# Norms on column strips, totals by transposes, decay exponents without a mask product

## The chip, the cores and the metric

The kernel runs on one core of one Trainium2 chip. The metric is device time in microseconds, the median of the runs of one build. A core has TensorE (matmul, PE in the profile, with its weight loads as PEld), VectorE (DVE), ScalarE (ACT), GpSimd (POOL) and SyncE (SP, which issues most transfers here). Each engine works through its own instructions in order, and the engines wait for each other by semaphores.

## The reference

One layer of a hybrid backbone: 1024 latent tokens and 256 context tokens of width 1024. All that the change touches lies in the modulation and in the gated delta rule.

```python
mod_x = silu(c) @ w_ada + b_ada                     # six vectors of 1024: shift, scale, gate, twice
px = modulate(rms_norm(x), sh1, sc1) @ w_in         # one projection, columns split into two groups
...
q = l2_normalize(silu(conv(q))) * 128 ** -0.5       # 4 heads of 128
k = l2_normalize(silu(conv(k)))
gam = cumsum(g)                                     # per chunk, per direction
decay = exp(where(tril, gam[:, None] - gam[None, :], -inf))
a_mat = eye + where(strict, (beta * k) @ k.T * decay, 0)
u, w = solve(a_mat, v * beta), solve(a_mat, k * beta * exp(gam))
qk = where(tril, q @ k.T * decay, 0)
o = (q * exp(gam)) @ S + qk @ (u - w @ S)           # scanned over chunks, forward and backward, summed
...
x = x + g1 * (concat(delta, neighbourhood_attention) @ w_out)
x = x + g2 * (silu(gate) * up) @ w_ffn_out          # gate, up from modulate(rms_norm(x), sh2, sc2) @ w_ffn_in
```

Here `tril` is the lower triangle of a chunk, and for the backward scan the upper one.

## The kernel before, in words

Every large product is made of three products of split operands in a fast 32-bit format (high by high, high by low, low by high), into 128x512 banks of the accumulator: `mm_part` (L422) for the projection, L1418 and L1761 for the feed-forward part.

**Order.** From about 150 to 500 us the program goes through a list of projection blocks (q, k, v of the delta rule, nq and nk of the attention, wide blocks for the rest). Between the main products of a block it steps generators that carry all other work in pieces: `modulation`, `block_inverses`, `preps`, and the `norm` and `finish` of the block before. A scheduler with a cost model of its own then decides the final order on each engine, within the data dependences; a few instructions are pinned by `keep_in_program_order`. So an edit in one place can shift rows in another. Three more stages follow: the scan with attention (500 to 775 us), the output projection and the feed-forward part.

**Modulation.** For each of eight groups of 512 columns, VectorE adds up eight scaled tiles of weights into `acc2` (128x512, L238). `reduce` (L220 to L225) then sums over the 128 partitions with four matmuls of one moving column, and VectorE adds the bias. Four groups run in the projection stage, two at about 826 us, two between 1175 and 1245 us.

**A query block's norm (L500 to L507).** The squares `r` (128 x 1024) are summed over partitions by eight matmuls that have 128 squares' columns as stationary operand and a column of ones as moving one, which gives the sums with tokens on partitions; VectorE copies them to `SQ`.

**A query block's finish (L558 to L583).** The transposed keys are loaded from DRAM into `kTh`, the products of keys and queries of each chunk are made on TensorE (L570), ScalarE copies them to `kk` (L571), and one store puts them into `qk_d` (L583), unmasked.

**preps (L970 to L1070).** For each of ten chunk numbers, a pair of chunks (one for each direction) is worked on. `fetch` loads the keys' products `kk` (L991), the inverses' blocks `xc` (L992) and the query products `at` (L996). `prep` makes the exponents' operands `rg` on VectorE (L1008), copies blocks to `fx` on ScalarE (L1012), multiplies with the triangles on TensorE (L1020, two products), adds a third product that brings −1e30 to every position outside the triangle (L1023), and takes the exponential `e` (L1028). Masked positions of `e` are thus zero, and VectorE multiplies `kk` and `at` by it (L1031, L1036). GpSimd copies blocks into `y` (L1034); TensorE multiplies with `fx` (L1044) and then, block row by block row, with `y` (L1055).

The buffers of `preps` take the memory of the block inverses, so the first `rg` waits until the last of the inverses (`ut` and `WK`, L952 to L957) has been stored to `x_d`.

Of the kernel before, what the change touches and what calls it, by code (L numbers as in the profile page):

```python
# [88 lines left out]
def hybrid(ctx, tc, a, dbg):  # L89
# [15 lines left out]
    def lasting(name, shape, dt=F32):  # L105
        return persist.tile(shape, dt, name=name, tag=name)

    prm = lasting("prm", [128, 64])
    ones = lasting("ones", [128, 128])
    bias = lasting("bias", [128, 8])  # L110
    modp = lasting("modp", [128, 48])
# [11 lines left out]
    act.dma_start(sel, a["sel"])  # L123
    cst = const("cst", [128, NCONST])
    M = [cst[:, i * 128:(i + 1) * 128] for i in range(4)] + [ones]
    mc = [cst[:, 512 + i * 32:512 + (i + 1) * 32] for i in range(4)]
    ident = M[C_ID]
    n1w, n2w, bada = prm[:, 0:8], prm[:, 8:16], prm[:, 16:64]
# [7 lines left out]
    b_eps, b_naq = bias[:, 0:1], bias[:, 1:2]  # L136
    mr = const("mr", [128, 5, 128], F32R)

# [5 lines left out]
    kk_d = dram.tile([128, NCH, 4, 128], F32, name="kk_d", tag="kk_d")  # L144
    qk_d = dram.tile([128, 8, 4, 128], F32, name="qk_d", tag="qk_d")
    nv_d = dram.tile([T, 512], F32, name="nv_d", tag="nv_d")
# [61 lines left out]
    def modulation(adp, qs, bank, bufs=4, sums=2):  # L208
# [11 lines left out]
        def reduce(q, acc2):  # L220
            p = bank()
            for b in range(4):
                pe.matmul(p[:, b:b + 1], acc2[:, b * 128:(b + 1) * 128], ones[:, 0:1], start=True, stop=True)  # L223
            s = slice(16 + q * 4, 20 + q * 4)
            dve.tensor_tensor(modp[:, s], p[:, 0:4], bada[:, s], OP.add)  # L225

# [165 lines left out]
    with ExitStack() as bs:  # L392
# [32 lines left out]
        class Block:  # L425
# [64 lines left out]
            def norm(self):  # L490
# [8 lines left out]
                if kind == "q":  # L499
                    sp.dma_start(qT_d[:, :, i], acc[:, t0:].rearrange("p (c t) -> p c t", t=128))  # L500
                    p = bank()
                    for c in range(8):
                        m = pe.matmul(p[:, c:c + 1], r[:, t0 + c * 128:t0 + (c + 1) * 128], M[C_ONE][:, 0:1],
                                      start=True, stop=True)
                        if not c:
                            tc.keep_in_program_order(m)
                    dve.tensor_copy(SQ[:, :, i], p[:, 0:8])  # L507
                    return
# [30 lines left out]
            def finish(self):  # L539
# [22 lines left out]
                if kind in "kq":  # L562
# [10 lines left out]
                    if kind == "k":  # L573
# [4 lines left out]
                        for b in range(4):  # L578
                            s = slice(b * 32, b * 32 + 32)
                            pool.tensor_copy(KKc.rearrange("p (c h) i -> p c h i", h=4)[s, :, i], kk[s, :, s])  # L580
                            pool.memset(kk[s, :, s], 0.0)
                    dst = kk_d if kind == "k" else qk_d
                    sp.dma_start(dst[:, :, i], kk[:, c0:])  # L583

# [90 lines left out]
        with ExitStack() as xs:  # L675
# [18 lines left out]
            for j in range(3):  # L694
                load_ada(j)
            sp.dma_start(cst, a["cst"])
            sp.dma_start(masks, a["masks"])
# [43 lines left out]
            with tc.manual_schedule(engines={mybir.EngineType.PE, mybir.EngineType.DVE, mybir.EngineType.Activation}):  # L741
# [40 lines left out]
                for k in range(1, KT):  # L782
                    if k == 3:
                        ascope.close()
                        h_tiles(pools(bs, "hp2", "right"), 4)
                    if k + 1 < KT:
                        normed_tile(k + 1)
                    for j, b in enumerate(first):
                        b.mm([k])
                        for q in AHEAD.get((k, j), ()):  # L790
                            if q in rows:
                                column(q)
                            else:
                                ada(q, act.copy)
                    if k == 5:
                        act.copy(mr[:, 4], ident)
                        act.copy(mr[:, 0:4], masks)
# [4 lines left out]
        adp = pools(late, "adp", "left")  # L802
        mneg = adp.tile([128, 2, 128], F32R, name="mneg", tag="mneg")
        for d in range(2):
            act.mul(mneg[:, d], mr[:, d].bitcast(F32), -1.0e30)
        first_half = ExitStack()
# [161 lines left out]
        def preps():  # L968

            first_half.close()  # L970
            with ExitStack() as gs:
# [13 lines left out]
                def fetch(i):  # L985

                    got = []
                    for d in range(2):
                        c = ORDER[d][i]
                        kk, xc = work("kk", 6), pp.tile([128, 2, 4, 32], F32, name="xc", tag="xc", bufs=4)  # L990
                        sp.dma_start(kk, kk_d[:, c])  # L991
                        sp.dma_start(xc, x_d[:, d, :, c * 4:c * 4 + 4])  # L992
                        at = None
                        if c >= 2:
                            at = work("at", 4)
                            sp.dma_start(at, qk_d[:, c - 2])  # L996
                        got.append((d, c, kk, xc, at))
                    return i, got

                def prep(i, got):  # L1000
# [16 lines left out]
                    for d, c, kk, xc, at in got:  # L1017
                        p = bank("pr")
                        for j in range(2):
                            m = pe.matmul(p, mr[:, d], fl(rgs[2 * d + j]), start=j == 0, stop=False)  # L1020
                            if i == 0:
                                tc.keep_in_program_order(m)
                        pe.matmul(p, mr[:, 4], mneg[:, d].rearrange("p (o i) -> p o i", o=1).to_broadcast(  # L1023
                            [128, 4, 128]), start=False, stop=True)
                        e = work("e", 2)
# [818 lines left out]
```

## Time and profile before

| | us |
| --- | --- |
| median of three runs (smallest, largest) | 1490.75 (1489.34, 1491.34) |
| profiled execution | 1493.29 |
| its span, first to last instruction | 1491.4 |
| TensorE busy | 1454.2 |
| VectorE busy | 997.8 |
| ScalarE busy | 706.0 |
| GpSimd busy | 92.4 |

The mean granted TensorE clock is 0.997. A "record" is one TensorE instruction of the trace: a matmul of ordinary 32-bit numbers leaves two, a transpose or a product in the fast format one. Matmuls are pipelined, so a duration reaches into the next instruction's.

### The profile page before, as it was taken

How to read it: one execution, taken by the hardware profiler on the slowest of the kernel's cores; microseconds unless marked ns; L12 is line 12 of the kernel's file. 1: busy time of each engine (PE TensorE's matmuls, PEld its weight loads, DVE VectorE, ACT ScalarE, POOL GpSimd, SP SyncE). 2: the span in 40 equal slices, each digit the busy share in tenths (PEclk: the TensorE clock that was granted, in tenths of full speed). 3: DMA queues.
4: the chain of work that ended last, by engine and by line, in shares of the span. 5: the costliest groups of instructions: out<-in, count | busy, mean ns of one | idle time of the engine just before them, and what ended most of it. 6: DMA issues, size and time to landing. Idle time of an engine off the chain costs nothing. (4 is left out here: it accounts for less than half of the span.)

```text
span 1491.4 us, 23615 instructions
## 1 busy us (share of the span) xinstructions
PE 1454.2 (98%) x8708; PEld 1223.5 (82%) x8708; DVE 997.8 (67%) x1794; ACT 706.0 (47%) x1388; POOL 92.4 (6%) x168
## 2 busy tenths in 40 slices
PE   6999999999999989989999999999999999999998
PEld 3889898887898878888878888888888888888887
DVE  5783698865663547779966589755556556698652
ACT  5453544457653256667752374333333335355440
POOL 1033000202110001001100000000000000000000
PEclk9999999999999999999999999999999999999999
DMA  9265232877654489986349105333233335898742
GB/s 386 77 208 162 74 86 66 267 241 239 207 182 159 140 271 294 291 249 213 116 168 312 43 15 198 120 106 106 107 106 106 100 106 182 292 330 289 254 135 85
DMA packets 203091, 264.19 MB, mean 177 GB/s; under 512 B 15712, under 2 KB 111456, under 8 KB 201952
## 3 DMA queue, kind: packets, MB, share of 16 engines
q1 hardware_dynamic: 195376, 256.87, 53.2%
q10 hardware_dynamic: 7600, 5.81, 1.2%
q8 instruction: 69, 1.13, 0.3%
q14 instruction: 46, 0.38, 0.1%
HBM read 197.87 MB, written 68.94 MB: 179 GB/s over the span
## 5 line engine op out<-in xcount | busy, mean ns | idle before, releaser
L1479 ACT CAST uhi<-wq 128x512 fp32r<-128x512 f32 x101 | 61.3, 622 | 134.0 <-issue 84.7
L1479 ACT CAST uhi<-ws 128x512 fp32r<-128x512 f32 x91 | 54.0, 621 | 146.6 <-PE ps L1418 96.7
L422 PE MATMUL blk<-hh,whi 128*128 128x512 f32 (+1 forms) x410 | 120.3, 387 | 0.5 <-ACT kk L571 0.5
L422 PE MATMUL blk<-hl,whi 128*128 128x512 f32 (+1 forms) x410 | 114.3, 371 | 0.3 <-DVE hl L738 0.3
L618 PE MATMUL blk<-zw,hh 128*128 128x256 f32 (+1 forms) x576 | 112.6, 289 | 1.0 <-ACT cr L470 1.0
L422 PE MATMUL blk<-hh,wlo 128*128 128x512 f32 (+1 forms) x410 | 112.5, 369 | 0.0
L1480 DVE TENSOR_TENSOR ulo<-wq,uhi 128x512 fp32r<-128x512 f32 x101 | 67.9, 687 | 58.5 <-ACT uhi L1479 31.9
L1418 PE MATMUL ps<-hT,uhi 128*128 128x512 f32 x336 | 103.7, 390 | 0.0
L1418 PE MATMUL ps<-hT,ulo 128*128 128x512 f32 x336 | 103.5, 389 | 0.0
L1418 PE MATMUL ps<-lT,uhi 128*128 128x512 f32 x336 | 103.4, 389 | 0.0
L618 PEld LDWEIGHTS blk<-zw,hh 128*128 128x128 f32 x576 | 90.9, 189 | 4.1 <-ACT cr L470 1.4
L1418 PE MATMUL ps<-hB,uhi 128*128 128x512 f32 x288 | 89.1, 390 | 0.0
L1418 PE MATMUL ps<-lB,uhi 128*128 128x512 f32 x288 | 88.7, 389 | 0.0
L1418 PE MATMUL ps<-hB,ulo 128*128 128x512 f32 x288 | 88.7, 389 | 0.0
L422 PEld LDWEIGHTS blk<-hl,whi 128*128 128x128 f32 x410 | 71.2, 189 | 14.2 <-DVE hl L738 0.8
L422 PEld LDWEIGHTS blk<-hh,wlo 128*128 128x128 f32 x410 | 71.1, 188 | 13.7
L618 PE MATMUL blk<-zw,hl 128*128 128x256 f32 (+1 forms) x288 | 81.8, 284 | 0.0
L422 PEld LDWEIGHTS blk<-hh,whi 128*128 128x128 f32 x410 | 67.5, 190 | 15.4 <-issue 4.0
L1418 PEld LDWEIGHTS ps<-hT,ulo 128*128 128x128 f32 x336 | 63.1, 188 | 13.1
L1418 PEld LDWEIGHTS ps<-lT,uhi 128*128 128x128 f32 x336 | 63.1, 188 | 13.1
L1418 PEld LDWEIGHTS ps<-hT,uhi 128*128 128x128 f32 x336 | 62.9, 188 | 13.0
L316 DVE CUSTOM_DVE_ANT_0 ex<-sc,bt 128x640 f32<-128x640 f32 x64 | 52.5, 820 | 22.9 <-PE sc L310 17.5
(361 smaller groups left out, 3357.4 us busy)
## 6 DMA issues: line engine op xcount, KB each, us to landing
wq<-w_fo SPq DMA_DIRECT2D x99, 256.0 KB, 4.0
wq<-w_gu SPq DMA_DIRECT2D x88, 256.0 KB, 2.8
wad<-wa SPq DMA_DIRECT2D x64, 256.0 KB, 4.4
t_d<-g SPq DMA_DIRECT2D x22, 512.0 KB, 3.5
fr<-t_d SPq DMA_DIRECT2D x44, 256.0 KB, 5.0
bt<-rpb SPq DMA_DIRECT2D x48, 192.0 KB, 3.9
f_d<-g SPq DMA_DIRECT2D x33, 256.0 KB, 2.1
fr<-f_d SPq DMA_DIRECT2D x33, 256.0 KB, 4.1
```

The costliest lines, as they stand in the source:

```text
L316: dve.tensor_tensor_reduce(e, sc[:, u * 640:u * 640 + 640], bt, -1.0, 3.0e38, OP.add, OP.min, m[:, 0:1])
L422: pe.matmul(o, ww[:, k], xx[k][:, s], start=k == 0 and j == 0, stop=k == KT - 1 and j == 2)
L618: pe.matmul(p[:, :c1 - c0], x[k][:, s], ww[:, k, c0:c1], start=k == 0 and j == 0, stop=k == KT - 1 and j == 2)
L1418: pe.matmul(o, w[wi][:, k], x[xi][:, k], start=first and k == 0 and j == 0, stop=k == n - 1 and j == 2, skip_group_check=True)
L1479: act.copy(hi, self.raw[key])
L1480: dve.tensor_tensor(lo, self.raw[key], hi.bitcast(F32), OP.subtract)
```

## The change

**Totals.** Four transposes of `acc2` go into one 128x512 bank, VectorE sums each transposed block along its free axis into `modp`, and then adds the bias.

**Query norms.** Four matmuls have a 128x32 block of ones as stationary and 256 columns of squares as moving operand; each writes to another strip of 32 partitions of one bank. ScalarE copies the bank's first 256 columns to a buffer, two transposes bring the tokens onto partitions, and VectorE copies every 32nd column to `SQ`.

**Decays.** The third product and its operands are gone. The exponent is then zero outside the triangle, and `e` is one there. So what `e` multiplies has to be zero there already: three memsets per `kk` tile in `fetch` clear the 32-wide blocks outside the triangle (60 in all; the diagonal blocks were cleared before, by `finish` of the key blocks), and `finish` of the query blocks makes two masked copies of the products, for the forward direction into the `kTh` buffer and for the backward one in place, and stores both.

**The identity** gets a tile of its own with its own load, in persistent memory; the table of constants shrinks by as much.

```diff
         def reduce(q, acc2):
             p = bank()
             for b in range(4):
-                pe.matmul(p[:, b:b + 1], acc2[:, b * 128:(b + 1) * 128], ones[:, 0:1], start=True, stop=True)
+                pe.transpose(p[:, b * 128:(b + 1) * 128], acc2[:, b * 128:(b + 1) * 128], ident)
             s = slice(16 + q * 4, 20 + q * 4)
-            dve.tensor_tensor(modp[:, s], p[:, 0:4], bada[:, s], OP.add)
+            dve.tensor_reduce(modp[:, s], p.rearrange("p (b j) -> p b j", b=4), AX.X, OP.add)
+            dve.tensor_tensor(modp[:, s], modp[:, s], bada[:, s], OP.add)
...
                     p = bank()
-                    for c in range(8):
-                        m = pe.matmul(p[:, c:c + 1], r[:, t0 + c * 128:t0 + (c + 1) * 128], M[C_ONE][:, 0:1],
-                                      start=True, stop=True)
+                    for c in range(4):
+                        m = pe.matmul(p[32 * c:32 * c + 32, :256], M[C_ONE][:, 0:32],
+                                      r[:, t0 + c * 256:t0 + (c + 1) * 256], start=True, stop=True)
                         if not c:
                             tc.keep_in_program_order(m)
-                    dve.tensor_copy(SQ[:, :, i], p[:, 0:8])
+                    row = cp.tile([128, 272], F32, name="zt", tag="zt", bufs=2)
+                    act.copy(row[:, :256], p[:, :256])
+                    p = bank()
+                    for b in range(2):
+                        pe.transpose(p[:, b * 128:b * 128 + 128], row[:, b * 128:b * 128 + 128], ident)
+                    dve.tensor_copy(SQ[:, :, i].rearrange("p (s b) -> p s b", b=2),
+                                    p[:, :256].rearrange("p (b s j) -> p s b j", b=2, s=4)[:, :, :, 0])
                     return
...
-                    dst = kk_d if kind == "k" else qk_d
-                    sp.dma_start(dst[:, :, i], kk[:, c0:])
+                    if kind == "k":
+                        sp.dma_start(kk_d[:, :, i], kk)
+                        return
+                    for d, x in enumerate((kT.rearrange("p (c t) -> p c t", t=128), kk)):
+                        keep = M[C_LE + d].rearrange("p (o i) -> p o i", o=1).to_broadcast([128, NCH - c0, 128])
+                        dve.tensor_tensor(x[:, c0:], kk[:, c0:], keep, OP.mult)
+                        sp.dma_start(qk_d[d, :, :, i], x[:, c0:])
...
                         sp.dma_start(kk, kk_d[:, c])
+                        for b in range(3):
+                            rows, cols = (b, slice(32 * b + 32, 128)) if d else (b + 1, slice(0, 32 * b + 32))
+                            pool.memset(kk[q32[rows], :, cols], 0.0)
...
-                            sp.dma_start(at, qk_d[:, c - 2])
+                            sp.dma_start(at, qk_d[d, :, c - 2])
...
-                            m = pe.matmul(p, mr[:, d], fl(rgs[2 * d + j]), start=j == 0, stop=False)
+                            m = pe.matmul(p, mr[:, d], fl(rgs[2 * d + j]), start=j == 0, stop=j == 1)
                             if i == 0:
                                 tc.keep_in_program_order(m)
-                        pe.matmul(p, mr[:, 4], mneg[:, d].rearrange("p (o i) -> p o i", o=1).to_broadcast(
-                            [128, 4, 128]), start=False, stop=True)
```

The scheduler's order moves with it. TensorE before, at the first decays (L1020) of `preps`, 25 main products behind the second L570 group of the first query block. A row gives the line, the operation, out<-in, the shape, and how many follow each other:

```order
L422 MATMUL blk<-hh_131,whi 128x512
L1020 MATMUL pr<-rg,mr 128x512
L422 MATMUL blk<-hh_131,whi 128x512
L422 MATMUL blk<-hl_132,whi 128x512
L1020 MATMUL pr<-rg,mr 128x512
L1023 MATMUL pr<-mneg,mr 128x512
L1020 MATMUL pr<-rg,mr 128x512
L422 MATMUL blk<-hl_132,whi 128x512
L422 MATMUL blk<-hh_131,wlo 128x512
L1020 MATMUL pr<-rg,mr 128x512
L1023 MATMUL pr<-mneg,mr 128x512
```

The same place in the changed kernel (L422 is L423 there, L1020 is L1032):

```order
L423 MATMUL blk<-hh_467,wlo 128x512 x2
L1032 MATMUL pr<-rg,mr 128x512
L423 MATMUL blk<-hh_469,whi 128x512
L1032 MATMUL pr<-rg,mr 128x512
L423 MATMUL blk<-hh_469,whi 128x512
L423 MATMUL blk<-hl_470,whi 128x512
L1032 MATMUL pr<-rg,mr 128x512
L423 MATMUL blk<-hl_470,whi 128x512
L423 MATMUL blk<-hh_469,wlo 128x512
L1032 MATMUL pr<-rg,mr 128x512
```

The two mask products are gone, and the decays now stand 12 main products behind that L570 group in place of 25.

VectorE before, where the first `rg` is made (L478 is a tap of the convolution, L238 modulation's running sum, L507 the copy of a query norm):

```order
L507 COPY SQ<-m 128x8
L478 SCALAR_TENSOR_TENSOR cacc<-cr,cw,cacc 128x1023
L952 STREAM_TRANSPOSE ut<-WK 128x1280
L478 SCALAR_TENSOR_TENSOR cacc<-cr,cw,cacc 128x1023
L955 TENSOR_TENSOR WK<-WK,NB 128x1280
L478 SCALAR_TENSOR_TENSOR cacc<-cr,cw,cacc 128x1022
L238 SCALAR_TENSOR_TENSOR acc_2466<-wad,sc_100,acc_2466 128x512 x3
L1008 TENSOR_TENSOR rg<-GH,cst 128x512
```

And in the changed kernel (L478 is L479, L952 is L961, L1008 is L1020; the copy of the norm is L513):

```order
L961 STREAM_TRANSPOSE ut<-WK 128x1280
L479 SCALAR_TENSOR_TENSOR cacc<-cr,cw,cacc 128x1023
L964 TENSOR_TENSOR WK<-WK,NB 128x1280
L479 SCALAR_TENSOR_TENSOR cacc<-cr,cw,cacc 128x1023
L239 SCALAR_TENSOR_TENSOR acc_2465<-wad,sc_101,acc_2465 128x512
L1020 TENSOR_TENSOR rg<-GH,cst 128x512
L1020 TENSOR_TENSOR rg<-GL,cst 128x512
L1020 TENSOR_TENSOR rg<-GH,cst 128x512
L1020 TENSOR_TENSOR rg<-GL,cst 128x512
L479 SCALAR_TENSOR_TENSOR cacc<-cr,cw,cacc 128x1022
L513 COPY SQ<-m 128x8
L239 SCALAR_TENSOR_TENSOR acc_2465<-wad,sc_101,acc_2465 128x512
```

The copy of the norm and one tap no longer stand ahead of the transpose of the inverses, and two of the running sums ahead of `rg` are gone; two masked products of 128x1024 (L594) come soon behind.

GpSimd in the changed kernel, with buffer numbers, at the first pair of `preps` (before, only the copies to `y` stood there, which are L1034 before and L1044 now):

```order
L1044 COPY y00_2501<-xc_2512 32x4x32 x4
L1003 MEMSET kk_2511 32x4x32
L1003 MEMSET kk_2511 32x4x64
L1003 MEMSET kk_2511 32x4x96
L1003 MEMSET kk_2518 32x4x96
L1003 MEMSET kk_2518 32x4x64
L1003 MEMSET kk_2518 32x4x32
L1044 COPY y10_2502<-xc_2519 32x4x32 x4
```

Six memsets of two `kk` tiles stand between the copies of a pair.

More of the change, by code (lines that the diff above doesn't have):

```diff
@@ L109, in hybrid @@
     ones = lasting("ones", [128, 128])
+    ident = lasting("ident", [128, 128])
     bias = lasting("bias", [128, 8])
@@ L123, in hybrid @@
     act.dma_start(sel, a["sel"])
[L124 to L127, printed above, removed]
+    cst = const("cst", [128, NCONST - 128])
+    M = [ident] + [cst[:, i * 128:(i + 1) * 128] for i in range(3)] + [ones]
+    mc = [cst[:, 384 + i * 32:384 + (i + 1) * 32] for i in range(4)]
     n1w, n2w, bada = prm[:, 0:8], prm[:, 8:16], prm[:, 16:64]
@@ L136, in hybrid @@
     b_eps, b_naq = bias[:, 0:1], bias[:, 1:2]
-    mr = const("mr", [128, 5, 128], F32R)
+    mr = const("mr", [128, 4, 128], F32R)
     v_d = dram.tile([T, 512], F32, name="v_d", tag="v_d")
@@ L144, in hybrid @@
     kk_d = dram.tile([128, NCH, 4, 128], F32, name="kk_d", tag="kk_d")
-    qk_d = dram.tile([128, 8, 4, 128], F32, name="qk_d", tag="qk_d")
+    qk_d = dram.tile([2, 128, 8, 4, 128], F32, name="qk_d", tag="qk_d")
     nv_d = dram.tile([T, 512], F32, name="nv_d", tag="nv_d")
@@ L695, in hybrid @@
                 load_ada(j)
-            sp.dma_start(cst, a["cst"])
+            sp.dma_start(ident, a["cst"][:, 0:128])
+            sp.dma_start(cst, a["cst"][:, 128:])
             sp.dma_start(masks, a["masks"])
@@ L795, in hybrid @@
                     if k == 5:
-                        act.copy(mr[:, 4], ident)
                         act.copy(mr[:, 0:4], masks)
@@ L802, in hybrid @@
         adp = pools(late, "adp", "left")
-        mneg = adp.tile([128, 2, 128], F32R, name="mneg", tag="mneg")
-        for d in range(2):
-            act.mul(mneg[:, d], mr[:, d].bitcast(F32), -1.0e30)
         first_half = ExitStack()
```

## Prediction

> **What bounds the kernel now.** I read the page's first part, then the busy time by stage (one window per stage), then the timeline at the places that the change touches. The columns of a window row are: stretch, its length, busy us and instruction count of PE, weight loads, VectorE, ScalarE and GpSimd, granted clock, DMA share, GB/s.
>
> ```profile
> span 1491.4 us, 23615 instructions
> PE 1454.2 (98%) x8708; PEld 1223.5 (82%) x8708; DVE 997.8 (67%) x1794; ACT 706.0 (47%) x1388; POOL 92.4 (6%) x168
> 150.00:500.00 350.00, 350.00 (x2352) 296.20 (x2350) 241.85 (x326) 178.68 (x325) 36.76 (x88) 0.99 0.56 170
> 500.00:775.00 275.00, 256.28 (x2322) 226.33 (x2321) 193.95 (x555) 172.41 (x461) 25.98 (x36) 0.99 0.71 215
> ```
>
> TensorE sets the pace: 98% of the span, and 350.00 of 350.00 us in the stage that holds the whole change but four modulation totals. There a TensorE instruction taken away shortens the kernel by its issue interval, and work added to another engine costs nothing until TensorE waits for it. The scan stage has 18.7 us of TensorE idle time (275.00 − 256.28), but the change puts nothing in it except another order of the same instructions.
>
> **Mask products: removed.** The timeline rows are: start, duration, engine, line, operation, out<-in, count. Durations overlap, so I price by the distance between starts.
>
> ```profile
> L1023 PE MATMUL pr<-mneg,mr x20: 389/396/401, 281.6 to 456.6; 128*128 128x512 f32 x20
> 281.39 0.39 PE L1020 MATMUL pr<-rg,mr 128*128 128x512 f32 x1
> 281.62 0.40 PE L1023 MATMUL pr<-mneg,mr 128*128 128x512 f32 x1
> ```
>
> A 128x512 product takes 0.23 us of the engine's time (281.39 to 281.62), not its 0.396, and a pair 0.46. Twenty of them: 20 × 0.23 = **−4.6 us**.
>
> **Modulation totals: one-column products become transposes.** A total was four one-column matmuls, eight records.
>
> ```profile
> 260.00 0.95 PE L223 MATMUL m<-ones,acc 128*128 128x1 f32 x8
> 260.81 0.70 PE L422 MATMUL blk<-hl,whi 128*128 128x512 f32 x2
> 261.35 0.63 PE L422 MATMUL blk<-hh,wlo 128*128 128x512 f32 x2
> 78.58 1.25 PE L546 MATMUL m<-cst,cacc 128*128 128x128 f32 x10
> 79.59 0.48 PE L422 MATMUL blk<-hh,wlo 128*128 128x512 f32 x1
> 79.91 1.11 PE L570 MATMUL m<-cacc 128*128 128x128 f32 x8
> ```
>
> Before: 0.81 us (260.00 to 260.81), and the pair behind takes 0.54 (to 261.35) in place of 0.46, so 0.89. After: the ten transposes at 78.58 took 1.01, hence 0.10 each, and the product behind them 0.32 in place of 0.23, so 4 × 0.10 + 0.09 = 0.49. There are eight totals (four of them in the projection stage): 8 × 0.40 = **−3.2 us**.
>
> **Query norms on column strips.** A norm was eight one-column matmuls (16 records); it becomes four matmuls with a 32-column stationary and 256 moving columns, one for each strip of the output, then two transposes.
>
> ```profile
> 268.65 1.84 PE L503 MATMUL m<-ones,cr 128*128 128x1 f32 x16
> 270.35 0.72 PE L422 MATMUL blk<-hh,whi 128*128 128x512 f32 x2
> 270.91 0.63 PE L422 MATMUL blk<-hl,whi 128*128 128x512 f32 x2
> 24.96 1.07 PE L715 MATMUL pm<-wada,wide 128*32 128x256 f32 x16
> 25.96 0.73 PE L762 MATMUL pm<-whi 128*128 128x512 f32 x2
> 361.24 1.88 PE L511 MATMUL m<-cr,cst 128*128 128x512 f32 x4
> 294.74 0.44 PE L1055 MATMUL pr<-y,kk 128*32 128x32 f32 x8
> 295.11 0.73 PE L422 MATMUL blk<-hl,whi 128*128 128x512 f32 x2
> 295.68 0.62 PE L422 MATMUL blk<-hh,wlo 128*128 128x512 f32 x2
> ```
>
> Before: 1.70 (268.65 to 270.35), and 0.56 − 0.46 = 0.10 behind: 1.80. The nearest row to the new form is the kernel's own: sixteen records of 128x256 on 32-column strips took 1.00 us (24.96 to 25.96), so eight take 0.50. Entering and leaving a strip costs about 0.1 each (295.11 to 295.68 is 0.57 for a pair of 0.46), so 0.2. The two transposes take 0.2 and 0.09 behind. Sum 0.99, a gain of 0.8, four times: **−3.2 us**. Bounds: if the strips ran one behind another, four of 256 columns would take what the row at 361.24 took for two of 512, some 1.9, and with one change of form and the transposes 2.5 a norm (+2.8 in all, 6.0 worse than my term); without any cost of changing form, −4.0. I take the row of the same form.
>
> **The clock.** At one place two of these groups stand close together.
>
> ```profile
> 283.92 0.95 PE L223 MATMUL m<-ones,acc 128*128 128x1 f32 x8
> 285.51 2.29 PE L503 MATMUL m<-ones,cr 128*128 128x1 f32 x16
> 287.66 1.20 PE L422 MATMUL blk<-hh,whi 128*128 128x512 f32 x2
> 289.51 3.62 PE L1044 MATMUL pr<-fx,kk 128*128 128x128 f32 x16
> 293.06 0.63 PE L1055 MATMUL pr<-y,kk 128*32 128x32 f32 x8
> 293.62 0.73 PE L422 MATMUL blk<-hh,wlo 128*128 128x512 f32 x2
> 287.50:290.00 2.50, 2.50 (x9) 2.11 (x9) 2.50 (x4) 0.00 (x0) 2.38 (x3) 0.50 1.11 366
> 307.29 1.95 PE L1044 MATMUL pr<-fx,kk 128*128 128x128 f32 x16
> 75.00:82.50 7.50, 7.50 (x47) 6.54 (x46) 7.46 (x12) 5.21 (x7) 0.00 (x0) 1.00 0.42 125
> ```
>
> The engine counts as busy throughout, yet the granted clock falls to 0.50 behind a total and a norm 1.6 us apart; sixteen one-column records alone (268.65) leave it at full speed. The dip costs 2.15 − 1.70 = 0.45 in the norm, 1.85 − 0.92 = 0.93 in the four products from 287.66 to 289.51, 3.62 − 1.95 = 1.67 in L1044, and 0.56 − 0.37 = 0.19 in L1055 (293.06 to 293.62, against 294.74 to 295.11): 3.2 us. With wide moving operands in place of one-column ones I expect no dip: **−3.2 us**.
>
> [...]
>
> **A wait that appears.** The first decays' matmuls (L1020) move up TensorE's order, from 25 to 12 main products behind the first query block's last L570, so they come 13 × 0.23 = 3.0 us sooner, and 1.2 more for the total and the norm saved ahead: 280.71 − 4.2 = 276.5. Their operand rg waits on VectorE for a store to land:
>
> ```profile
> 270.52 0.17 DVE L507 COPY SQ<-m 128x8 f32<-128x8 f32 x1 [1.02 <-PE m L503]
> 271.80 1.50 DVE L952 STREAM_TRANSPOSE ut<-WK 128x1280 f32<-128x1280 f32 x1
> 279.51 0.69 DVE L1008 TENSOR_TENSOR rg<-GH,cst 128x512 fp32r<-128x512 f32 x1 [0.20 <-DMA x_d<-ut]
> 280.71 0.39 PE L1020 MATMUL pr<-rg,mr 128*128 128x512 f32 x1
> ```
>
> That chain starts sooner too: the copy of SQ, with its 1.02 us wait, and a convolution tap no longer stand ahead of the transpose, which a longer total offsets in part. I take 1.8 us, so rg is ready at 279.51 + 0.69 − 1.8 = 278.4, and TensorE, in order, waits 278.4 − 276.5 = **+1.9 us**. Bounds: 0 (chain early enough) and 3.7 (not earlier at all).
>
> **What is hidden.** Extra VectorE work comes to eight masked products of 128x1024 at about 1.2 us (9.8), nearest row the weight split L204; reductions and a copy are small. ScalarE, busy 49.96 of 90 us there, gets four copies. GpSimd gets 60 memsets.
>
> ```profile
> 255.00:345.00 90.00, 90.00 (x547) 75.61 (x546) 67.34 (x100) 49.96 (x86) 19.85 (x38) 0.96 0.82 248
> L204 DVE TENSOR_TENSOR wlo<-wraw,whi x26: 1206/1216/1310, 65.6 to 828.9; 128x1024 fp32r<-128x1024 f32 x26
> L581 POOL MEMSET kk<- x16: 354/358/362, 90.1 to 142.8; 32x320 f32 x16
> 361.83 3.68 POOL L1034 COPY y<-xc 32x128 f32<-32x128 f32 x8 [19.21 <-DMA y_d<-y]
> 367.61 0.45 PE L1055 MATMUL pr<-y,kk 128*32 128x32 f32 x16
> ```
>
> VectorE in the query stretch rises from 67.3 to about 79.5 with 2.4 us for four longer totals, and the stretch itself shortens to about 80.6. That is tight, but modulation's running sums need no deadline, and the weight splits are ready long before use. I take 0. If the cover is gone, a late wlo or rg stops TensorE: the rivals below. Six memsets a pair at 0.36 fit the 2.1 us between the y copies' end (365.51) and L1055 (367.61) once kk has landed. The extra store of queries and ident's own load are issued by SP, at 0 too: the stretch ran with a DMA share of 0.82.
>
> **Sum.** −4.6 − 3.2 − 3.2 = −11.0 on TensorE, −3.2 for the clock, +1.9 for the wait: −12.3 us. It is made on the profiled run (span 1491.4, time 1493.3, 1.9 outside), 2.5 above the median. I apply it to the median: 1490.75 − 12.3 = 1478.45, so **1478.5 us**.
>
> **Rivals.**
> - The dip stays, or comes at another place, as the transposes still let the clock fall: 3.2 not gained, 1481.7. For: only two transposes and short strips replace the norm. Against: clock 1.00 from 75.00. Chance 0.20.
> - No new wait: rg is early, 1476.6. For: the chain lost its 1.02 us wait. Chance 0.15.
> - VectorE loses part: some of its idle time cannot be used, and TensorE waits some 7 us more, 1486. For: 79.5 in 80.6. Chance 0.10.
> - The strips don't overlap, so that part does not do what it says: 6.0 worse, 1484.5. Against: the row at 24.96. Chance 0.05.
> - **Slower:** VectorE becomes the pace-setter of the query stretch. If it kept all of its 22.7 us of idle time there (90.00 − 67.34), it would need 79.5 + 22.7 = 102.2 against 80.6: +21.6, in place of the 1.9, so −14.2 + 21.6 = +7.4, 1498. It decides once more than some 14 us of that idle time cannot be closed. Against: the sums L238 can wait. Chance 0.05.
>
> Something else 0.03; my forecast 0.42.
>
> **How the numbers follow.** A measurement of this kernel can tell 0.2%, 3 us, so faster is below 1487.8. The forecast, the first, second and fourth rival are faster, and half of the third: 0.87. Within 0.2% 0.07, slower 0.06. The range: bounds of the wait give 1476.6 to 1480.3; no cost of changing form with no wait 1475.8; the dip 1481.7; strips 1484.5; VectorE's part 1486. I take 1474 to 1486; the likeliest case's own is 1475.5 to 1480.5.
>
> **What would show it.** TensorE instructions down by about 20 + 8 × 4 + 4 × 6 = 76; L1020's group without mask products between; totals 0.40 to the next start; strips 0.5; granted clock 1.00 all through 270 to 300; a gap of 0 to 3.7 us ahead of the first decays, released by rg. It would be wrong if window rows between 255 and 345 show TensorE idle behind wlo, rg or kk, if the idle time of the scan stage moves by more than 3 us through its new order, or if y copies behind the memsets end after L1055's turn.

## Result, and the profile after

The changed kernel takes 1480.51 us (median of 6 runs, 1478.93 to 1481.61) against 1489.62 for the kernel before (6 runs): ratio 0.9939, 95% interval 0.9928 to 0.9951, or 9.1 us less. A second comparison (below) gave 1478.65 against 1489.95, ratio 0.9931 (0.9918 to 0.9943). One of its five runs of the changed kernel took 8172.25 us at a granted clock of 1.00, for a reason that no trace shows, and is left out of the ratio; the other four took 1477.94 to 1479.45. The prediction was 1478.5, in a range of 1474 to 1486. So the time was right; of the terms behind it some were not.

The page of the kernel after, first lines, and the windows by stage (columns as in the prediction: stretch, length, busy time of PE, weight loads, VectorE, ScalarE, GpSimd, granted clock, DMA share, GB/s):

```profile
span 1479.8 us, 23576 instructions
PE 1442.2 (97%) x8632; PEld 1206.7 (82%) x8632; DVE 1011.7 (68%) x1810; ACT 706.4 (48%) x1389; POOL 127.3 (9%) x228
150.00:500.00 350.00, 346.69 (x2334) 288.08 (x2333) 257.82 (x346) 181.45 (x332) 71.02 (x148) 1.00 0.59 182
255.00:345.00 90.00, 88.87 (x568) 69.80 (x569) 81.11 (x116) 56.42 (x103) 38.50 (x62) 1.00 0.92 277
284.00:294.00 10.00, 8.87 (x82) 6.44 (x82) 8.89 (x13) 8.75 (x22) 9.21 (x16) 1.00 1.06 321
```

TensorE lost 76 records (8708 to 8632), as counted beforehand. The clock is 1.00 from 284 to 294 us, where it was 0.66 before. VectorE's busy time between 255 and 345 us came to 81.1 us (79.5 forecast for the query stretch). And TensorE, which had no idle time between 150 and 500 us, now has 3.3 us of it (350.00 − 346.69). These are its waits there, by what ended them:

```profile
PE pr L1054 <- ACT fx L1024: 1.1, 1, 1.1
PE blk L630 <- ACT cr L471: 1.0, 1, 1.0
PE pr L1032 <- DVE y L1067: 0.5, 1, 0.5
PE pr L1065 <- POOL y L1044: 0.3, 1, 0.3
PE pr L1065 <- ACT kk L1057: 0.3, 1, 0.3
```

The wait at L630 stands behind the last main product, and was there before too, behind 500 us; the other four are new, and none of them is at `rg`.

I measure the projection stage from the first main product (first row below) to the last (second row): 33.7 to 505.3 before, 471.6 us; 33.1 to 496.6 after, 463.5 us. It is 8.1 us shorter.

```profile
L422 PE MATMUL blk<-hh,whi x410: 276/392/796, 33.7 to 504.1; 128*128 128x512 f32 x77, 128*128 128x256 f32 x60
L422 PE MATMUL blk<-hh,wlo x410: 277/390/502, 35.0 to 505.3; 128*128 128x512 f32 x76, 128*128 128x256 f32 x61
```

```profile
L423 PE MATMUL blk<-hh,whi x410: 276/392/792, 33.1 to 495.4; 128*128 128x512 f32 x77, 128*128 128x256 f32 x60
L423 PE MATMUL blk<-hh,wlo x410: 277/390/503, 34.4 to 496.6; 128*128 128x512 f32 x76, 128*128 128x256 f32 x61
```

The stages behind the scan (from the first product of the output projection, L1547, to the end) take 708.85 us before and 707.08 after, 1.8 us less; ten of the fourteen profiles agree with one of these lengths, that of their totals, to 0.05 us, and four are off by 0.2 to 0.8. The scan stage between (from the last main product to L1547) varies from one profile to the next by several us without any edit to it (277.3 us in the profile before, 276.1 after, 272.7 in a second profile of the changed kernel), so a single profile says nothing of 2 us there.

Summed over the stage, TensorE's intervals from start to start show what each part did. These are its new pieces, in the timeline of the kernel after (start, duration, engine, line, operation, out<-in, count):

```profile
323.38 0.61 PE L423 MATMUL blk<-hh,wlo 128*128 128x512 f32 x2
323.93 0.64 PE L504 MATMUL m<-cr,ones 128*32 128x256 f32 x8
324.49 0.73 PE L423 MATMUL blk<-hh,whi 128*128 128x512 f32 x2
325.06 0.40 PE L423 MATMUL blk<-hl,whi 128*128 128x512 f32 x1
325.30 0.38 PE L512 MATMUL m<-ident,zt 128*128 128x128 f32 x2
325.43 0.48 PE L423 MATMUL blk<-hl,whi 128*128 128x512 f32 x1
325.75 0.62 PE L423 MATMUL blk<-hh,wlo 128*128 128x512 f32 x2
339.34 0.60 PE L223 MATMUL m<-ident,acc 128*128 128x128 f32 x4
339.69 0.71 PE L423 MATMUL blk<-hh,whi 128*128 128x512 f32 x2
340.24 0.63 PE L423 MATMUL blk<-hl,whi 128*128 128x512 f32 x2
```

A norm's strips take 0.56 (323.93 to 324.49), with 0.09 in front and 0.11 behind for the change of form, its transposes 0.13 and 0.09: 0.98, against the forecast 0.99. So the four strips do run side by side. A total takes 0.35, and 0.09 behind: 0.44, against 0.49.

| part, in the projection stage | forecast, us | in this profile, us |
| --- | --- | --- |
| 20 mask products | −4.6 | −4.7 |
| four totals (of eight) | −1.6 | −1.9 |
| four norms | −3.2 | −3.1 |
| clock | −3.2 | −3.2 |
| stalls | +1.9 at `rg` | +4.8, none at `rg` |
| sum | −10.7 | −8.1 |

The sum on the right is measured, and the stalls are what the other lines leave: 8.1 − 12.9 = −4.8. Only 2.2 us of them stand in the table of waits. By distances between starts the same four places and two small gaps at `y` products come to some 3.0 us (at the first, below, 283.72 to 285.26 is 1.54 where a main product takes 0.23). The remaining 1.8 us I can't place; some of it may be the other order of the instructions and no stall at all.

### The profile page after: what moved, and what is told of

Same layout as the page of the kernel before. It is cut to its first block, busy times and chain, and to the rows that moved or that the text cites. A ratio compares the mean times of both kernels' runs of the same rounds, so it can differ in the third digit from the quotient of the medians.

```text
span 1479.8 us, 23576 instructions
## 1 busy us (share of the span) xinstructions
PE 1442.2 (97%) x8632; PEld 1206.7 (82%) x8632; DVE 1011.7 (68%) x1810; ACT 706.4 (48%) x1389; POOL 127.3 (9%) x228
## 5 line engine op out<-in xcount | busy, mean ns | idle before, releaser
L423 PE MATMUL blk<-hh,whi 128*128 128x512 f32 (+1 forms) x410 | 120.8, 387 | 0.5 <-ACT kk L578 0.5
L423 PE MATMUL blk<-hl,whi 128*128 128x512 f32 (+1 forms) x410 | 114.7, 371 | 0.3 <-DVE hl L751 0.3
L630 PE MATMUL blk<-zw,hh 128*128 128x256 f32 (+1 forms) x576 | 112.5, 289 | 2.3 <-DVE vt L557 1.2
L423 PE MATMUL blk<-hh,wlo 128*128 128x512 f32 (+1 forms) x410 | 112.9, 369 | 0.0
L630 PEld LDWEIGHTS blk<-zw,hh 128*128 128x128 f32 x576 | 91.0, 189 | 5.4 <-DVE vt L557 1.4
L423 PEld LDWEIGHTS blk<-hl,whi 128*128 128x128 f32 x410 | 71.1, 188 | 14.1 <-DVE hl L751 0.8
L423 PEld LDWEIGHTS blk<-hh,wlo 128*128 128x128 f32 x410 | 71.1, 188 | 13.8 <-issue 0.4
L630 PE MATMUL blk<-zw,hl 128*128 128x256 f32 (+1 forms) x288 | 82.1, 285 | 0.0
L423 PEld LDWEIGHTS blk<-hh,whi 128*128 128x128 f32 x410 | 67.5, 189 | 16.6 <-issue 5.3
L1490 DVE TENSOR_TENSOR ulo<-ws,uhi 128x512 fp32r<-128x512 f32 x91 | 59.9, 685 | 12.5 <-PE ps L1771 8.0
```

What stands on the lines that cost most here:

```text
L423: pe.matmul(o, ww[:, k], xx[k][:, s], start=k == 0 and j == 0, stop=k == KT - 1 and j == 2)
L630: pe.matmul(p[:, :c1 - c0], x[k][:, s], ww[:, k, c0:c1], start=k == 0 and j == 0, stop=k == KT - 1 and j == 2)
L1490: dve.tensor_tensor(lo, self.raw[key], hi.bitcast(F32), OP.subtract)
```

## Experiments

Each kernel ran beside the kernel before on the same chip: three jobs on three chips, of four kernels each. "Clock lost" is 1490 us × (1 − mean granted clock), averaged over the runs; the clock is listed to 0.001 per run, so only averages are used. It counts lost clock anywhere in the kernel, in the scan stage too. "Stage" is the projection stage's length in the one profiled run, measured as above (471.6 before, 463.5 after).

| kernel | median, before beside it | ratio (95% interval) | clock lost (before) | stage |
| --- | --- | --- | --- | --- |
| totals alone | 1483.59, 1490.46 | 0.9961 (0.9947 to 0.9975) | 1.2 (3.7) | 466.5 |
| norms alone | 1485.50, 1490.46 | 0.9975 (0.9965 to 0.9985) | 2.3 (3.7) | 466.1 |
| decays alone | 1485.98, 1490.46 | 0.9973 (0.9962 to 0.9984) | 2.4 (3.7) | 468.8 |
| before, totals apart | 1487.43, 1490.46 | 0.9985 (0.9972 to 0.9997) | 2.7 (3.7) | 467.5 |
| after, no clearing | 1481.69, 1488.59 | 0.9950 (0.9937 to 0.9964) | 2.1 (2.6) | 466.1 |
| after, first pair later | 1481.65, 1488.59 | 0.9952 (0.9940 to 0.9965) | 1.2 (2.6) | 464.6 |
| before, totals moved | 1489.68, 1488.59 | 1.0014 (1.0003 to 1.0026) | 3.8 (2.6) | 469.4 |
| after, two stores of keys | 1493.54, 1488.59 | 1.0035 (1.0023 to 1.0048) | 8.1 (2.6) | 476.5 |
| after, again | 1478.65, 1489.95 | 0.9931 (0.9918 to 0.9943) | 0.0 (3.0) | 463.7 |
| after, an extra step | 1491.22, 1489.95 | 1.0012 (1.0002 to 1.0021) | 8.0 (3.0) | 461.7 |
| first pair later, transposes later | 1481.17, 1489.95 | 0.9947 (0.9934 to 0.9960) | 0.6 (3.0) | 464.0 |
| all three | 1488.52, 1489.95 | 0.9998 (0.9988 to 1.0009) | 7.3 (3.0) | 461.0 |

### Totals alone

The kernel before with the first two blocks of the diff (`reduce`, and the identity in its own tile).

> The kernel before with the totals alone by transposes (and the identity in its own tile). The second total still stands right ahead of a norm of 16 one-column records. Theory, one-column records standing close together bring the clock down: the dip ends, so 8 totals x 0.45 us and 3.2 us for the dip, -6.8 us, and the granted clock is 1.00 from 270 to 300 us. [...]

It came out at −6.9 us. The second total, now transposes, still stands right ahead of a norm of 16 one-column records, and the clock is not brought down. Timeline, and the window that answers to it:

```profile
283.12 0.60 PE L223 MATMUL m<-ident,acc 128*128 128x128 f32 x4
283.56 1.84 PE L504 MATMUL m<-ones,cr 128*128 128x1 f32 x16
285.26 0.71 PE L423 MATMUL blk<-hh,whi 128*128 128x512 f32 x2
286.04 1.95 PE L1046 MATMUL pr<-fx,kk 128*128 128x128 f32 x16
284.00:294.00 10.00, 10.00 (x91) 8.81 (x91) 9.04 (x14) 7.18 (x20) 7.41 (x12) 1.00 0.88 277
```

The norm takes 1.70 in place of 2.15, and L1046 1.95 in place of 3.62. The stage is 5.1 us shorter: 1.9 for four totals and 3.2 for the clock, with no stall.

### Norms alone

The block `norm` of the diff alone.

> The kernel before with the query norms alone on column strips. Theory: 4 norms x 0.8 us and the dip's 3.2 us, -6.4 us, clock 1.00 from 270 to 300 us. Rival, the dip stays since the total ahead of the norm is still one of eight one-column records: -3.2 us. Rival, strips run one behind another: +2.8 us less what the dip gives.

The time fell by 5.0 us by the medians (2.2 to 5.2 by the ratio's interval), between the two theories. The profiled run is clear: the clock is 1.00 through the place of the dip (284 to 294 us), and the stage is 5.5 us shorter, which is 3.1 for the norms and 3.2 for the clock less 0.8 that went into stalls, 0.6 of them at `rg`. Over all runs, though, 2.3 us of clock were still lost where the totals alone had left 1.2. In this profile that loss lies in the scan stage (half-clock stretches from 525.4 and from 634.6 us), where no total and no norm stands. Strips that run one behind another are excluded.

### Decays alone

The rest of the diff, without totals, norms and the identity's tile.

> The kernel before with the decays' part alone (no mask products, 60 memsets, masked products of the queries stored by direction). Totals and norms are one-column products as before and stand side by side at the same place. Theory: 20 products x 0.233 = -4.7 us on TensorE, the dip stays, and the waits for fx and y that the changed kernel shows (about 2.7 us) come with this part, so -2 us. Rival, the waits come from the time saved in norms and totals and not from the new work of VectorE and GpSimd: -4.7 us. Rival, VectorE sets the pace between 255 and 345 us: 0 or slower.

−4.5 us by the medians, −2.9 if the lost clock is taken off both sides (1490.1 − 3.7 and 1485.9 − 2.4, means). The stage says where: it is 2.8 us shorter, though the 20 products took 4.7 with them and the dip lasted 3.4 us in place of 6.8, worth another 1.6. So 3.5 us of stalls come with this part alone (4.7 + 1.6 − 2.8). The row of the dip, before and with the decays alone, and then the waits:

```profile
284.00:294.00 10.00, 10.00 (x58) 9.16 (x57) 7.09 (x9) 4.82 (x13) 7.94 (x13) 0.66 0.95 299
```

```profile
284.00:294.00 10.00, 10.00 (x64) 9.01 (x63) 9.24 (x11) 3.95 (x12) 9.00 (x18) 0.83 1.02 310
PE pr L1057 <- ACT kk L1049: 1.2, 2, 1.0
PE pr L1057 <- POOL y L1036: 0.5, 1, 0.5
```

So stalls come with this part alone, as the first theory said; the rival, that all of them come from time saved in norms and totals, fails, since those are as before here. But they are not the changed kernel's stalls: the waits stand at 384.8, 385.2 and 408.5 us, and there is none at the first pair's product with `fx`, the longest one in the changed kernel, where the clock still falls here. With 0.8 in the norms' version, at `rg`, and none in the totals' one, the parts' stalls add up to 4.3 of the 4.8 us; the amounts add up, the places don't.

### Before, with the totals apart

```diff
-                for _ in range(4):
+                for _ in range(8):
                     yield
                 reduce(q, prev)
```

> The kernel before, nothing removed: the totals of the projection stage are made eight steps behind their sums in place of four, so that no total stands within 2.7 us of a norm. Theory, a total and a norm of one-column records close together bring the clock down: the clock is 1.00 from 255 to 345 us and the time falls by 3.2 us. Rival, the fall of the clock has another cause at that place: the dip stays, and the time changes by less than 1 us.

−3.0 us, and in the profiled run no dip between 284 and 294 us:

```profile
284.00:294.00 10.00, 10.00 (x94) 8.62 (x92) 9.91 (x13) 6.80 (x18) 7.84 (x10) 1.00 0.82 245
```

The stage is 4.1 us shorter: 3.2 for the dip, and 0.9 for a better place of the other pieces. So this profile bears the theory out. Over the twelve runs the clock lost is 2.7 us, 1.0 less than the 3.7 of the kernel before beside it, and this doesn't speak against the theory: in this profile 5.1 us were lost, all of it in the scan stage (half clock from 525.8 to 529.2 and from 635.1 to 641.9 us), where nothing was moved on purpose. The average takes in both stages.

### Before, with the totals moved

The same edit with 6 in place of 8.

> The kernel before with the projection stage's totals six steps behind their sums in place of four: no total stands next to the second norm any more, but the third stands directly behind the fourth norm (at about 330 us). Nothing is removed. Theory, a total and a norm of one-column records next to each other bring the clock down wherever they stand: no dip at 285 us, one at about 333 us, and as the work behind it there is as dense, the time is within 1.5 us of the kernel before. Rival, the dip belongs to the work around 285 us: no dip at either place, -3 us.

This fits neither theory. The third total stands directly behind the fourth norm (328.44 behind 326.74, eight and sixteen one-column records), and the clock is 1.00 there and at 285 us:

```profile
326.74 1.84 PE L503 MATMUL m<-ones,cr 128*128 128x1 f32 x16
328.44 1.03 PE L223 MATMUL m<-ones,acc 128*128 128x1 f32 x8
284.00:294.00 10.00, 10.00 (x81) 8.77 (x80) 6.77 (x9) 7.33 (x18) 4.21 (x12) 1.00 0.90 256
325.00:345.00 20.00, 20.00 (x114) 16.82 (x113) 15.59 (x34) 12.87 (x22) 3.70 (x8) 1.00 0.87 272
```

Yet the eleven runs lost 3.8 us of clock on average, against 2.6 for the kernel before beside them, and took 1.1 us more; the one half-clock stretch of this profile is in the scan stage, from 635.8 us. So a total and a norm side by side do not bring the clock down each time; why not here, no run shows.

### After, without the clearing

```diff
                         sp.dma_start(kk, kk_d[:, c])
-                        for b in range(3):
-                            rows, cols = (b, slice(32 * b + 32, 128)) if d else (b + 1, slice(0, 32 * b + 32))
-                            pool.memset(kk[q32[rows], :, cols], 0.0)
```

> The changed kernel without the 60 memsets on GpSimd; TensorE's order stays the same row by row. Left out: the clearing of the keys' products outside the triangle, so the solve works on other numbers. Theory, GpSimd's memsets ahead of the copies to y delay the y products: the waits of TensorE ahead of L1044 and L1055 (in this kernel's numbering) for y fall by about 1.5 us, and the time by as much, to 11 to 12 us below the kernel before. Rival, the memsets are hidden and the waits come from ScalarE's and VectorE's queues: within 0.5 us of the changed kernel in the projection stage, 9 to 10 us below the kernel before.

Leaving the memsets out does not shorten the stage. With the same order on TensorE, it is 466.1 us, 2.6 longer than with them; 1.7 of that is a half-clock stretch at the first pair (0.83 from 284 to 294 us), and without it the stage would be 464.4, still no shorter. TensorE waits at the same sixteen products, shorter ahead of the first eight (one chunk), longer ahead of the rest (the other chunk):

```profile
284.38 1.13 PE L1051 MATMUL pr<-fx,kk 128*128 128x128 f32 x8 [0.29 <-POOL y L1041]
286.94 2.00 PE L1051 MATMUL pr<-fx,kk 128*128 128x128 f32 x8 [1.43 <-issue]
```

The first chunk's products start 0.88 us earlier than in the changed kernel (285.26), so the memsets did hold them up there. The second chunk's now wait for ScalarE's copies of `fx`, the last of which ends at 286.84, 0.10 ahead of them.

### After, first pair later

```diff
-                LATE, stores, tick = 7, [], [0]
+                LATE, stores, tick = 9, [], [0]
```

> The changed kernel with the first pair's decays nine steps behind its start in place of seven: 12 more main products stand ahead of the first decays and 10 to 14 more ahead of the first product with fx. Nothing is removed. Theory, TensorE came too early at the first fx product (1.06 us of wait) and at the decays and y products behind it: these waits go and the projection stage gets 1.5 to 2.5 us shorter than the changed kernel's, 11 to 12 us below the kernel before. Rival, the later start only moves the waits to the second pair: no difference from the changed kernel.

The wait for `fx` went, and another came that is longer: two transposes of a norm now wait for ScalarE's copy of the strips.

```profile
289.19 0.44 PE L512 MATMUL m<-ident,zt 128*128 128x128 f32 x2 [2.10 <-ACT zt L509]
```

The stage is 1.1 us longer than the changed kernel's. The rival was right that the wait only moves, though not to the second pair.

### First pair later, transposes later

In addition, the two transposes and the copy to `SQ` move from `norm` to `finish`, behind the load of `kTh`.

> The kernel with the later first pair, and the two transposes of a query norm moved from the norm to the finish of the block, some main products later. Theory, in the version with the later first pair TensorE's 2.1 us wait for ScalarE's copy of the strips cancelled what the later start won: without it the projection stage is 2 us shorter than that version's 464.6, about 462.5. Rival, ScalarE's queue is late for all that waits on it, and the wait turns up at the next consumer: 464 us or more.

The wait for ScalarE's copy falls from 2.1 to 1.5 and does not go; the stage is 464.0. This speaks for the rival. In the changed kernel ScalarE is nearly full at this place: between 280.3 and 293.3 us it was busy for 12.16 of 13.00 us, against 7.75 in the kernel before (first row).

```profile
280.30:293.30 13.00, 13.00 (x69) 11.60 (x68) 10.59 (x13) 7.75 (x19) 9.71 (x14) 0.75 0.92 292
```

```profile
280.30:293.30 13.00, 11.87 (x95) 8.62 (x94) 11.08 (x16) 12.16 (x28) 11.87 (x21) 1.00 0.96 290
```

Since TensorE comes sooner, the evacuations, activations, `fx` copies and the new strip copy of this place fall together, and here three engines beside TensorE are over 85% busy at once. Being full is not what held up the strips' copy in the two versions with the later first pair, though: there ScalarE was busy 8.94 and 9.82 of the same 13.00 us. With the later first pair alone (TensorE's strips had ended at 285.04):

```profile
285.21 1.26 ACT L1024 COPY fx<-xc 32x128 f32<-32x128 f32 x4 [1.07 <-DMA xc<-x_d]
288.75 0.38 ACT L509 COPY zt<-m 128x256 f32<-128x256 f32 x1
```

The copy stands in ScalarE's order behind `fx` copies that wait 1.07 us for a transfer to land (0.24 in the other version), a table load of 1.28 us and two exponentials.

### After, two stores of the keys

The keys' products are stored masked by direction too (`kk_d` gets a leading 2, eight more VectorE products of 128x1280 in `finish` of the key blocks), and the memsets are left out.

> The changed kernel with the keys' products stored masked by direction too (eight more VectorE products of 128x1280 and four more stores of 640 KB, between 80 and 145 us), so that the 60 memsets are not needed; TensorE's order stays the same, and the result is the reference's. Theory: as without the memsets, 11 to 12 us below the kernel before, if VectorE has the 12 us to spare between 80 and 145 us (53 to 78 per cent busy there). Rival: the new products delay the weight splits there and cost what they bring, 7 to 10 us below.

It is slower than the kernel before. The stretch from 80 to 145 us had no room: TensorE waited 4.75 us there for one weight split, and behind it, at 154 to 159 us, 4.2 us for a decay table.

```profile
106.05 0.39 PE L646 MATMUL blk<-hh,zw 128*16 128x256 f32 x1 [4.75 <-ACT zw L620]
100.00:115.00 15.00, 10.25 (x65) 8.53 (x64) 12.78 (x17) 6.55 (x10) 7.12 (x9) 0.77 0.68 209
```

And the clock falls with the wait (0.77 in this window). A mean VectorE share of 53 to 78% did not mean that 12 us were to spare. How VectorE's products led to that wait is not shown: the split is ScalarE's, and had itself waited 1.63 us for its weights to land.

### After, again

The changed kernel, unaltered.

> The changed kernel once more, unaltered, beside the kernel before on one chip. In the first comparison the kernel before lost about 3 us a run to half-clock windows (mean granted clock 0.9975 and 0.9983 on two chips, x 1490) and the changed one 0.3 us. Theory, the clock's share of the gain is real and lasts: again about -9 us, with a mean clock of 0.999 or more. Rival, the few disturbed windows were luck of six runs: mean clock 0.998 as before the change, and only -6.4 us.

−11.3 us by the medians, no clock lost, and the stage 463.7 us, 0.2 from the first profile; the clock's share of the gain is there again. The wait at the first pair's product with `fx` is 1.1 us again, but is put down to VectorE's product of `kk` and `e` (L1041) and not to ScalarE's `fx`.

### After, an extra step

One more `yield 1` between the exponential and the products with `fx`, in every pair.

> The changed kernel with one more step of the background work between the exponential of a pair of chunks and the pair's products with fx, so that some six more main products stand between them from the third pair on; nothing is removed. Theory, TensorE's savings have shortened the cover of a chain of fixed length (exponential, product on VectorE, fx, y), and it stalls there: the stalls at 347, 359, 361 and 380 us (0.64, 0.51, 0.22 and 0.51 us) go, the projection stage is about 1.5 to 2 us shorter than the changed kernel's 463.5. Rival, the chain moves along and stalls as much: 463 to 464 us.

The stage is 1.8 us shorter, as the theory said, but for another reason, and the kernel is 12.6 us slower than the changed one. The waits at the later `y` products are gone from the list, and others stand in their place: 1.7 us at the first pair's product with `fx` and 2.0 at a later pair's decay. The last pair's products with `y` are now left behind the last main product, with nothing to cover their chain:

```profile
495.03 0.75 PE L423 MATMUL blk<-hh,wlo 128*128 128x256 f32 x3
495.71 0.59 PE L1066 MATMUL pr<-y,kk 128*32 128x32 f32 x16
502.78 1.06 PE L1066 MATMUL pr<-y,kk 128*32 128x64 f32 x16 [6.47 <-DVE y L1068]
```

About 2 us of work thus left the stage by my way of measuring it, so the stage got no shorter, and the clock came down in the idle time behind it as well: half clock from 499.9 to 510.1 us, 5.1 of the 8.5 us lost in this profile (8.0 on average). The test does not decide on the later pairs' stalls.

### All three

> The changed kernel with all three: a later first pair, the transposes moved, and the extra step. Theory, the stalls of the first pair and of the later ones are separate and add: projection stage 460.5 to 461.5 us, 2 to 3 us shorter than the changed kernel's, and 11 to 12 us below the kernel before. Rival: no shorter than the better of the two single versions.

It came to the same end: stage 461.0 by that measure, the same wait of 6.5 us behind it, and no gain at all in time. No version beat the changed kernel.

## Why the prediction was right, and where it was wrong

**What bounds the kernel, and the price of a TensorE instruction, were right.** Pricing by the distance between starts gave the masks (−4.6, measured −4.7), the norms (−3.2, measured −3.1) and, a little low, the totals: I took 0.40 a total and the rows give 0.45, so the term "eight totals, −3.2" should have been −3.7 (1.9 in the projection stage, 1.8 behind the scan). The transposes cost 0.09 each in a group of four (0.35), not the 0.10 taken from the group of ten.

**The clock's term came true at its place, and the averages that seem to confirm it are in part luck.** In the projection stage of the profile before, a half-clock stretch of 6.8 us cost 3.2 us, and it is gone in both profiles of the changed kernel. The term −3.2 was this one dip. The same profile has another, which I had not looked at, in the scan stage (0.50 from 638.3 to 641.7 us), behind 3.40 us of which TensorE was busy for 0.97:

```profile
286.70:293.50 6.80, 6.80 (x34) 6.19 (x34) 4.47 (x5) 2.54 (x8) 6.22 (x11) 0.50 1.03 328
634.90:638.30 3.40, 0.97 (x9) 0.78 (x7) 1.05 (x5) 2.81 (x5) 0.00 (x0) 1.00 1.07 321
638.30:641.70 3.40, 3.29 (x15) 2.97 (x16) 2.09 (x4) 3.06 (x8) 0.00 (x0) 0.50 0.57 137
```

Over 68 runs on three chips the kernel before lost 3.2 us on average (3.7, 2.6 and 3.0 by chip), the changed one 0.25 in its first comparison and nothing in its second. That this difference, too, is about 3.2 is luck: the average counts the scan stage's dips, which the forecast left out. Of the six profiled kernels that kept one-column groups only two (the kernel before, decays alone) lost clock in the projection stage, and five lost 1.7 to 5.1 us in the scan stage. Why the changed kernel loses less there I can't say; the changed kernel's first profile has one half-clock stretch there (0.50 from 542.4 to 545.7 us), its second none. Nor does taking the groups away suffice: without the clearing, 2.1 us were lost, and with the later first pair 1.2, in kernels that have no one-column group.

The rival that the dip stays is refuted by the changed kernel's runs. In the profile with the totals alone, four transposes, 0.44 us, right ahead of sixteen one-column records left the clock at 1.00 from 284 to 294 us.

My picture, that a total and a norm of one-column records close together bring the clock down, fits four other profiles: the kernel before (0.50 from 286.7 to 293.5 us), the decays alone (total at 285.87, norm at 286.70, 0.83 from 284 to 294 us), the norms alone and the totals apart (1.00 there in both). It does not fit the totals moved, where norm and total side by side, from 326.74 to 329.33 us, left the clock at 1.00. What sets that case apart is not shown, and six profiles would be no proof even of a picture that fits them all.

**The step that failed is "A wait that appears".** I placed +1.9 us at `rg` and held all else hidden. In the changed kernel TensorE waited for nothing at `rg`. It came at 275.91, as early as I had said (276.5), but the chain ahead of `rg` was early too:

```profile
268.91 1.50 DVE L961 STREAM_TRANSPOSE ut<-WK 128x1280 f32<-128x1280 f32 x1
275.01 0.69 DVE L1020 TENSOR_TENSOR rg<-GH,cst 128x512 fp32r<-128x512 f32 x1 [0.16 <-DMA x_d<-ut]
275.91 0.40 PE L1032 MATMUL pr<-rg,mr 128*128 128x512 f32 x1
```

The transpose moved up 2.9 us, where I took 1.8, and its store landed 6.1 us behind the transpose's start in place of 7.7. So that rival (no new wait, 1476.6) had the mechanism right at this place. The stalls came one step behind, at the pair's product with `fx` and its `y` products, and in later pairs:

```profile
283.72 0.48 PE L423 MATMUL blk<-hh,wlo 128*128 128x512 f32 x1
285.26 2.17 PE L1054 MATMUL pr<-fx,kk 128*128 128x128 f32 x16 [1.06 <-ACT fx L1024]
```

In all this is 4.8 us by the sum, of which 3.0 can be placed. At the first pair two chains release TensorE at almost the same time. In one, VectorE stands idle until GpSimd's memsets have cleared `kk`, then multiplies `kk` by `e`, and TensorE's first product starts 0.14 us behind the end of that (285.12); the other is ScalarE's second group of `fx` copies, which come behind a table load, an activation and a weight split (3.3 us of ScalarE's order).

```profile
284.43 0.69 DVE L1041 TENSOR_TENSOR kk<-kk,e 128x512 f32<-128x512 f32 x1 [1.24 <-POOL kk L1003]
284.89 1.25 ACT L1024 COPY fx<-xc 32x128 f32<-32x128 f32 x4
```

For the second chunk both chains end at about 286.15 (VectorE's product runs from 285.46 to 286.15). So taking away the memsets alone left the `fx` copies, and a later first pair left ScalarE's copy of the strips. I had put the 60 memsets and ScalarE's four new copies down as free, the one on the strength of their durations and the other of 49.96 busy us in 90; neither says behind what an instruction stands in its engine's order. TensorE idle behind `kk` between 255 and 345 us was among my signs of being wrong, and it came (1.1 us). ScalarE's first `fx` copies had themselves waited 1.47 us for `xc` to land from `x_d`; a version with these loads earlier was not run. For the stalls of later pairs (0.2 to 0.6 us each between 345 and 380 us) I have no cause that a run shows; VectorE's masked products are not among them, as they are done by then (the last starts at 332.2 us), and the loss of the mask products as cover for a chain of fixed length was not settled by the extra step.

**The rivals.** VectorE as the pace-setter did not come, though its busy time was as forecast. The strips overlap. The slower side found no support in the change itself; two of the experiments (two stores, extra step) show how near it is.

**The sum.** −12.3 was forecast; two comparisons gave −9.1 and −11.3. With the measured terms the sum is −4.7 − 3.7 − 3.1 − 3.2 + 4.8 = −9.9, between the two: the stalls took 2.9 more than I gave them, and the totals gave 0.5 back. The rest is variation between runs; the two profiles of the changed kernel differ by 3.1 us in all, and by 3.5 in the scan stage.

## What to carry to other kernels

Where TensorE is busy all the time, price a removed instruction by the distance between starts, and then ask of every chain that was hidden what its slack was: each us that TensorE saves ahead of it is taken from that slack, and a stage's mean busy share (ScalarE 50 of 90 us) doesn't show what an instruction stands behind in its engine's order. When the granted clock differs between two kernels, compare its mean over many runs, and see in the profiles in which stage the half-clock stretches lie before you credit an edit with them.

## What the runs showed of the hardware

In the kernel before, a group of 16 one-column 32-bit records took 1.70 us (268.65 to 270.35). In the changed kernel, four strips of 128x32 stationary by 256 moving columns took 0.56 us together, where four in a row would have taken an estimated 1.9, by the two 512-column products of L511 in the prediction. Going into that form cost 0.09 us, and coming out 0.11.

The clock: in the profile before it was 0.50 from 286.7 to 293.5 us, with TensorE busy for 6.80 of these 6.80 us, behind a total and a norm of one-column records that start 1.59 us apart (283.92 and 285.51). Two long waits of TensorE came with a lower clock. With two stores, the wait of 4.75 us ended at 106.05 us, and the clock was 0.77 from 100 to 115 us, where the changed kernel has 1.00; with the extra step, the wait of 6.47 us ended at 502.78 us, and the clock was at half from 499.9 to 510.1 us. The wait of 2.10 us with the later first pair, which ended at 289.19 us, left it at 1.00 from 280.3 to 293.3 us.
